# The first half-step of a decoder block on x with features on partitions: the norm's roots moved from x to the products' results

## The chip, the cores and the metric

The kernel runs on one core of a Trainium2 chip. The metric is the device time of one execution in microseconds (us). Times come from three runs of the kernel before and from one profiled execution of it. TensorE multiplies (PE, with PEld its weight loads), VectorE is DVE, ScalarE is ACT, GpSimd is POOL, and SyncE (SP) issues most transfers.

## The reference

One decoder block on x of 1024 tokens by 1024 features, float32. Only its first half-step is touched by the change:

```python
def rms_norm(x, g):
    y = xf * lax.rsqrt(jnp.mean(xf * xf, axis=-1, keepdims=True) + RMS_EPS)
    return y * g

def swiglu(x, w1, w3, w2):
    return (jax.nn.silu(x @ w1) * (x @ w3)) @ w2

# h = x + 1/2 * swiglu(rms_norm(x, g1), w1a, w3a, w2a)     D = 1024, D_FF = 2816
# then: u = rms_norm(h, g2) @ W_in, attention and pooling, gates, W_o, a second half-step, a last norm
```

The root of a token's mean square is one number for each token. It can be applied to the token's row of x, or, since `x @ w` is linear, to the results for that token.

## The kernel before

Every product is float32 split in two parts (high and low, type fp32r), three matmuls for one: high by high, high by low, low by high (`three`, `Sevens.product`). A product of 512 x 512 x 512 is 12 matmuls of 128x128 by 128x512.

The up-projections of a half-step are done with seven products in place of eight (`Quad`, L336): a pair of column blocks of w1 (A) and w3 (B) times x gives four quarters from seven products, numbered 1 to 7. Each takes one sum of x's quarters: `b11`, `b21`, `b22` (quarters of normed x by halves of tokens and of features), and `t1` to `t4`, sums of quarters. `Quad.operand` (L349) sums the weight's quarters on VectorE and splits the result: ACT writes the high part, GpSimd (or, for each third one, VectorE) the low part (`split`, L318). `Quad.run` (L388) issues the 12 matmuls; products 1 and 2 of a quad add up in one PSUM bank, 3 and 5 in another. `Pair.a_out` and `Pair.b_out` (L600, L629) take the results: for A the function (`Silu`) on ACT, for B the multiplication into A's result on VectorE. There are 11 pairs.

Normed x must have its features on partitions for the products. `begin_up1` (L981) loads rows of x (tokens on partitions), takes squares on ACT (`squares`), the inverse root on VectorE and GpSimd (`inverse`, a power of -0.5), scales the rows on VectorE, and turns them on TensorE, four 128x128 transposes into one bank (`Rows`, L402, and `turned`, L487). From the bank, ACT writes the high part and VectorE the low part. The gains are turned too (`gains`), and so are the roots (`means`).

While the first rows come, four products of the later pairs 4 and 5 (`led`) run on a first quarter of x that comes from memory with features on partitions already (`x_t`, unscaled but for the gain), and their results are scaled (`led_scaled`), stored and fetched when pairs 4 and 5 need them. Then come products 1 and 2 of pairs 0 to 2, with the transposes of rows 4 to 7 between them (`Entry.run`). After this opening, `up` (L696) runs products 6, 7, 5, 4 and 3 of the pairs begun, and then the pairs 3 to 10; an operand is prepared two products ahead.

The opening and the first part of `up` stand under `tc.manual_schedule()`: each engine has its instructions in the order of the code, written out by hand. The pairs 3 to 9 are ordered by the planner. SP's queue issues the transfers in the order of `load_all` and of `raws.load`.

`Down.add` (L871) adds the results of the down-projection to h with a factor of plus or minus one half.

Of the kernel before, what the change touches and what calls it, by code (L numbers as in the profile page):

```python
# [16 lines left out]
P = 128  # L17
# [120 lines left out]
def tile_block(  # L138
# [53 lines left out]
    consts.tile([P, 24], F32, name="pad")  # L192
# [3 lines left out]
    consts.tile([P, 32], F32, name="pad2")  # L196
# [87 lines left out]
    def scaled_part(t, c, gain):  # L284
        ve.scalar_tensor_tensor(h[t][:, c], h[t][:, c], inv[t][:, 1:2], gain[:, c], op0=OP.mult, op1=OP.mult)

# [19 lines left out]
    class Sevens:  # L306


        def __init__(self, name, X, fw, fs=None):
            self.name, self.X, self.fw, self.fs = name, X, fw, fs or fw  # L310
            self.n_lo = 0
            self.terms = (0, 1, 2)
            self.led = {}
# [251 lines left out]
    class Pair:  # L565
# [3 lines left out]
        def __init__(self, sv, j, sums, early=False, spare=False):  # L569
# [3 lines left out]
            self.place_of = [h_tile if spare else tmp, h_tile if early else tmp]  # L573
            self.u2 = (lambda n: h_tile(f"u2_{n}")[:, :HALF]) if spare else (lambda n: sv.half_tile("u", n))
# [5 lines left out]

        def place(self, row, cols):
            while len(self.y) <= row:
                self.y.append(self.place_of[len(self.y)](f"y_{self.sv.name}{self.j}_{len(self.y)}"))
            return self.y[row][:, cols]
# [5 lines left out]
        def fetch_b(self):  # L590
            if self.led is not None:
                self.u[2] = self.u2(f"{self.j}2")
                nc.sync.dma_start(self.u[2], self.led[1])

# [6 lines left out]
        def a_out(self, m, p):  # L601
            lows, highs = slice(0, HALF), slice(HALF, S)

            u2 = self.place(0, highs)
            if m == 1:
# [3 lines left out]
            elif m == 2:  # L609
                c = self.place(0, lows)  # L610
                if self.led is not None:
                    ve.tensor_tensor(c, p, u2, op=OP.add)
                    p = c
                ac.activation(c, p, AF.Silu)
            elif m == 7:
                ve.tensor_tensor(self.place(1, lows), p, u2, op=OP.add)
            elif m == 5:
                c22 = self.place(1, highs)
                ve.tensor_tensor(c22, p, self.place(1, lows), op=OP.add)
                ac.activation(c22, c22, AF.Silu)  # L620
            elif m == 4:
                u3 = self.place(1, lows)
                ve.scalar_tensor_tensor(u3, p, -1.0, u3, op0=OP.mult, op1=OP.add)
                ac.activation(u3, u3, AF.Silu)
            else:
                ve.tensor_tensor(u2, p, u2, op=OP.add)
                ac.activation(u2, u2, AF.Silu)

        def b_out(self, m, p):  # L629
            lows, highs = slice(0, HALF), slice(HALF, S)  # L630
            u, j = self.u, self.j
            if m == 1:
# [24 lines left out]
            else:  # L657
                ve.tensor_tensor(u[2], p, u[2], op=OP.add)
                d = self.place(0, highs)
                ve.tensor_tensor(d, d, u[2], op=OP.mult)  # L660

# [116 lines left out]
    class Down:  # L778
# [3 lines left out]
        def __init__(self, name, sums, half_tile, pair):  # L782
# [7 lines left out]
            self.right, self.apart = {}, set()  # L790
            downs.append(self)
# [137 lines left out]
    X = sums_of_x(scope.enter_context(sbuf("x1")), "f1", SUMS)  # L929

    for t in range(NT):
        h.append(h_tile(f"x{t}"))

    def load_rows(*ts):
        for t in ts:
            nc.sync.dma_start(h[t], x[t * P:(t + 1) * P, :])

    gain_row = keep.tile([P, D], F32, tag="gain", bufs=1, name="gain_ffn1")
    led_x, led_in = [], []
    for n in range(2):  # L940
        led_x.append(row(f"led_x{n}").rearrange("p (k c) -> p k c", k=2))
        led_in.append(row(f"led_w{n}").rearrange("p (k c) -> p k c", k=2))
    square = X["t1"][0][:, 0:2, :].rearrange("p k c -> p (k c)")
    square2 = tmp("square2")

    LED = (4, 5)
    led_dram = [dram.tile([P, HALF], F32, name=f"led{q}") for q in range(4)]

    def load_all():
        def features(kk):  # L950
            nc.sync.dma_start(led_x[kk], x_t[0, kk])

        def weight(q):
            nc.sync.dma_start(led_in[q // 2][:, q % 2], (w1a, w3a)[q % 2][2 * LED[q // 2]][:, LOWS])

        features(0)
        weight(0)
        weight(1)
        features(1)
        load_rows(0)  # L960
        weight(2)
        load_rows(1)
        weight(3)
        load_rows(2, 3)
        raws.depth = 2
        raws.load()
        load_rows(4)
        raws.depth = 3
        raws.load()
# [1541 lines left out]
```

## Time and profile before

| | us |
|---|---|
| median of 3 runs | 1884.19 (1883.82 to 1884.75) |
| profiled execution | 1884.1 |
| its span | 1882.3 |
| TensorE busy in the span | 1872.2 (99%) |
| VectorE busy | 1349.0 (72%) |
| ACT busy | 773.4 (41%) |
| GpSimd busy | 727.7 (39%) |

The span is what the profiler sees of the program; the rest of the time lies around it. A busy TensorE is one with matmuls in flight, whose ends are modelled; the start-to-start distance of matmuls tells their rate. Idle time of the other engines matters only where TensorE waits for them.

### The profile page before, as it was taken

The numbers are of one execution on the slowest core, as the hardware profiler recorded it, in microseconds if no ns is written. First come the engines' busy times: TensorE is split into PE (matmuls) and PEld (weight loads), VectorE is DVE, ScalarE is ACT, GpSimd is POOL, SyncE is SP. The second block draws the span as 40 slices with busy tenths as digits, with TensorE's granted clock in tenths as the row PEclk, the third lists the DMA queues.
The fourth block names the chain that finished last, engine by engine and source line by source line (L and its number), as shares of the span: only waits on it lengthen the run. The fifth ranks groups of instructions, "written<-read, shape, count | busy, mean of one in ns | idle before, by whom it ended". The sixth has DMA issues, their size and how long they took to land.

```text
span 1882.3 us, 24614 instructions
## 1 busy us (share of the span) xinstructions
PE 1872.2 (99%) x8758; PEld 1554.8 (83%) x8758; DVE 1349.0 (72%) x1981; ACT 773.4 (41%) x1395; POOL 727.7 (39%) x543
## 2 busy tenths in 40 slices
PE   9999999999999999999999999999999999999998
PEld 8888888888888888888888888888888888888886
DVE  7877666558786776658885897787765566577867
ACT  7433333334344543334445772363333333334344
POOL 4533333331223364444554457545333333312221
PEclk9999999999999999999999999999999999999999
DMA  6154323336565526765578878634332233354654
GB/s 248 56 201 163 128 100 116 115 118 222 177 224 196 182 91 221 243 219 188 209 254 315 313 227 294 262 147 172 125 139 85 89 107 111 136 200 156 225 197 146
DMA packets 146035, 334.98 MB, mean 178 GB/s; under 512 B 17784, under 2 KB 39288, under 8 KB 144376
## 3 DMA queue, kind: packets, MB, share of 16 engines
q1 hardware_dynamic: 142168, 322.55, 49.7%
q10 hardware_dynamic: 3744, 10.85, 1.6%
q8 instruction: 69, 1.13, 0.2%
q14 instruction: 54, 0.44, 0.1%
HBM read 232.76 MB, written 100.60 MB: 177 GB/s over the span
## 4 chain that ended last, share of the span: by engine, by line
PE 54%; DVE 3%; ACT 2%; issue 1%; DMA 1%; POOL 1%; ACTq 0%; SPq 0%; DVEq 0%; POOLq 0%
PE u_mixm L332 15%; PE d_f L869 8%; PE wo L2191 4%; PE yp L1933 1%; PE u_f20a L332 1%; PE u_f21b L332 1%; PE u_f20b L332 1%; PE u_f21a L332 1%; PE u_f210b L332 1%; PE u_f210a L332 1%; PE u_f29b L332 1%; PE u_f29a L332 1%; PE u_f28b L332 1%; PE u_f28a L332 1%; PE u_f27b L332 1%
## 5 line engine op out<-in xcount | busy, mean ns | idle before, releaser
L869 PE MATMUL d_f<-bhi_f,ahi_f 128*128 128x512 f32 x616 | 240.2, 390 | 0.0
L869 PE MATMUL d_f<-bhi_f,alo_f 128*128 128x512 f32 x616 | 239.7, 389 | 0.0
L869 PE MATMUL d_f<-blo_f,ahi_f 128*128 128x512 f32 x616 | 239.6, 389 | 0.0
L826 POOL TENSOR_TENSOR alo_f<-g_f,ahi_f 128x512 fp32r<-128x512 f32 x60 | 86.0, 1450 | 273.6 <-ACT ahi_f L822 273.6
L332 PE MATMUL u_mixm<-xhi_t_mix,wc_mixm 128*128 128x512 f32 x608 | 157.3, 391 | 0.6 <-ACT wc_mixm L320 0.6
L869 PEld LDWEIGHTS d_f<-bhi_f,ahi_f 128*128 128x128 f32 x616 | 115.7, 188 | 24.1 <-ACT h L422 0.5
L869 PEld LDWEIGHTS d_f<-bhi_f,alo_f 128*128 128x128 f32 x616 | 115.6, 188 | 24.1
L869 PEld LDWEIGHTS d_f<-blo_f,ahi_f 128*128 128x128 f32 x616 | 115.7, 188 | 23.9
L332 PEld LDWEIGHTS u_mixm<-xhi_t_mix,wc_mixm 128*128 128x128 f32 x608 | 113.5, 188 | 24.4 <-ACT wc_mixm L320 1.1
L332 PE MATMUL u_mixm<-xhi_b_mix,wc_mixm 128*128 128x512 f32 x456 | 120.3, 391 | 0.0
L323 POOL TENSOR_TENSOR wc_mixm<-s_mixm,wc_mixm 128x512 fp32r<-128x512 f32 x52 | 77.1, 1483 | 102.1 <-ACT wc_mixm L320 102.1
L332 PEld LDWEIGHTS u_mixm<-xhi_b_mix,wc_mixm 128*128 128x128 f32 x456 | 85.0, 188 | 17.2
L320 ACT ACTIVATE wc_mixm<-s_mixm 128x512 fp32r<-128x512 f32 x76 | 47.0, 628 | 112.2 <-DVE s_mixm L376 57.2
L822 ACT ACTIVATE ahi_f<-g_f 128x1024 fp32r<-128x1024 f32 x84 | 81.9, 975 | 4.1 <-DMA g_f<-gs_f 4.1
L332 PE MATMUL u_mixm<-xlo_t_mix,wc_mixm 128*128 128x512 f32 x304 | 81.3, 389 | 0.0
L323 POOL TENSOR_TENSOR wc_mixm<-raw,wc_mixm 128x512 fp32r<-128x512 f32 x41 | 62.3, 1523 | 37.5 <-ACT wc_mixm L320 31.8
L2191 PE MATMUL wo<-w_o,o_hi 128*128 128x512 f32 x224 | 69.4, 391 | 0.1
L822 ACT ACTIVATE bhi_f<-s_f2w 128x512 fp32r<-128x512 f32 x55 | 32.9, 628 | 86.7 <-DVE s_f2w L844 67.8
L822 ACT ACTIVATE bhi_f<-s_f1w 128x512 fp32r<-128x512 f32 x55 | 33.0, 629 | 83.1 <-DVE s_f1w L844 69.9
L332 PEld LDWEIGHTS u_mixm<-xlo_t_mix,wc_mixm 128*128 128x128 f32 x304 | 57.1, 188 | 12.0
L826 DVE TENSOR_TENSOR alo_f<-g_f,ahi_f 128x1024 fp32r<-128x1024 f32 (+1 forms) x48 | 57.6, 1200 | 8.5 <-ACT ahi_f L822 8.5
L332 PE MATMUL u_mixm<-xlo_b_mix,wc_mixm 128*128 128x512 f32 x228 | 61.0, 389 | 0.0
(1359 smaller groups left out, 4768.1 us busy)
## 6 DMA issues: line engine op xcount, KB each, us to landing
g_f<-gs_f SPq DMA_DIRECT2D x70, 512.0 KB
gs_f<-y_f SPq DMA_DIRECT2D x88, 256.0 KB
raw<-in_w2a_dram SPq DMA_DIRECT2D x35, 512.0 KB
raw<-in_w2b_dram SPq DMA_DIRECT2D x35, 512.0 KB
gs_f<-gb_f SPq DMA_DIRECT2D x46, 256.0 KB
raw<-in_w1a_dram SPq DMA_DIRECT2D x22, 512.0 KB
raw<-in_w3a_dram SPq DMA_DIRECT2D x22, 512.0 KB
raw<-in_w1b_dram SPq DMA_DIRECT2D x22, 512.0 KB
```

Source lines behind the costliest of these rows:

```text
L320: ac.activation(w[:, 0], src, AF.Copy)
L323: eng.tensor_tensor(w[:, 1], src, w[:, 0].bitcast(F32), op=OP.subtract)
L332: pe.matmul(p, a, b, start=(start and n == 0), stop=(n == 11), skip_group_check=not start)
L822: ac.activation(hi[:, c], src, AF.Copy)
L826: eng.tensor_tensor(lo[:, d], src[:, o], hi[:, d].bitcast(F32), op=OP.subtract)
L869: pe.matmul(self.banks[m][t], l, r, start=(first and q == 0), stop=(last and q == 2))
L1933: pe.matmul(p, a, b, start=(j == 0), stop=(j == 11))
L2191: pe.matmul(banks[m][t], l, r, start=(st == 0 and j == 0 and q == 0), stop=(st == 1 and j == 1 and q == 2))
```

## The change

All of x comes from memory with features on partitions (`x_t`, eight transfers). The opening makes the seven sums from it without the roots: gains are vectors of one number per partition (`gain1`, `less` is their negative). No row of x is turned any more. The rows of x are still loaded, into tiles of their own, for the squares alone. The roots of each half of the tokens are turned once (`spread`, four transposes into one bank) and copied to `norm`, a tile with a token's root in every partition. For the first factor (A) the results are multiplied with `norm`: product 2's on VectorE, the others on GpSimd (`lit`), and the function follows when the next result is taken (`late`, `functions`). For the second factor (B) nothing is multiplied; its roots go into the factor of one half in `Down.add` (`halves`). The four products led run later, behind the first products of pairs 0 and 1, unscaled, and are copied out by ACT. The gain of the next norm is loaded behind `up`.

```diff
         def a_out(self, m, p):
...
-                    p = c
-                ac.activation(c, p, AF.Silu)
+                    self.lit(c, lows)
+                elif self.sv.norm is not None:
+                    ve.tensor_tensor(c, p, self.sv.norm[:, lows], op=OP.mult)
+                    self.late.append(c)
...
-                ac.activation(c22, c22, AF.Silu)
+                self.lit(c22, highs)
...
+        def lit(self, c, cols):
+            if self.sv.norm is not None:
+                gp.tensor_tensor(c, c, self.sv.norm[:, cols], op=OP.mult)
+                self.late.append(c)
+            else:
+                ac.activation(c, c, AF.Silu)
...
         def add(self, m, t):
...
-                ve.scalar_tensor_tensor(hs, self.banks[m][t], 0.5 * sign, hs, op0=OP.mult, op1=OP.add)
+                by = 0.5 * sign
+                if self.halves is not None:
+                    by = self.halves[sign][:, 4 * th + t:4 * th + t + 1]
+                ve.scalar_tensor_tensor(hs, self.banks[m][t], by, hs, op0=OP.mult, op1=OP.add)
...
+        features(0, 0)
+        weight(0, LOWS)
+        weight(1, LOWS)
+        features(0, 1)
+        weight(2, LOWS)
+        weight(3, LOWS)
+        features(0, 2)
+        led_weight(0)
+        features(0, 3)
+        led_weight(1)
+        features(1, 2)
+        features(1, 0)
+        led_weight(2)
+        led_weight(3)
+        features(1, 3)
+        features(1, 1)
+        load_rows(0, 1)
+        weight(0, HIGHS)
+        load_rows(2, 3)
+        for j in (1, 2, 3):
+            weight(j, HIGHS)
+        more(6)
+        load_rows(4, 5, 6, 7)
...
+        def first_sum(k):
+            ve.tensor_tensor(xt(1, k), xt(1, k), xt(0, k), op=OP.subtract)
+
+        def scaled_b22(k):
+            ve.tensor_scalar(xt(1, k + 4), xt(1, k + 4), gain(k + 4), None, op0=OP.mult)
+            high("b22", k, xt(1, k + 4))
+        def second_sum(k):
+            t2[k] = bank("acc", f"x_t2_{k}")
+            ve.scalar_tensor_tensor(t2[k], xt(1, k), less[:, k:k + 1], xt(1, k + 4), op0=OP.mult, op1=OP.add)
+            high("t2", k, t2[k])
...
+        def out(n, m):
+            outs[n](m, banks[n])
+            pairs[n // 2].functions()
...
+        for k in (4, 5):
+            high("b21", k, xt(0, k), gain(k), ve if k == 5 else ac)
+            low("b21", k, xt(0, k), gain(k))
+        run(2, 1)
+        out(1, 1)
+        led_high(1)
+        for k in (6, 7):
+            high("b21", k, xt(0, k), gain(k), ve if k == 7 else ac)
+            low("b21", k, xt(0, k), gain(k))
+        run(3, 1)
+        out(2, 1)
+        led_high(2)
+        for k in (0, 1):
+            scaled_b22(k)
+            first_sum(k)
+        led_run(0)
+        out(3, 1)
+        led_high(3)
+        for k in (0, 1):
+            low("b22", k, xt(1, k + 4))
+        for k in (2, 3):
+            scaled_b22(k)
+            first_sum(k)
+        led_run(1)
+        led_out(0)
+        operand(0, 2)
+        for k in (2, 3):
+            low("b22", k, xt(1, k + 4))
+        squares_of_x(0)
+        squares_of_x(1)
+        led_run(2)
+        led_out(1)
+        operand(1, 2)
+        squares_of_x(2)
+        squares_of_x(3)
+        led_run(3)
+        for k in (0, 1):
+            second_sum(k)
+            low("t2", k, t2[k])
+            third_sum(k)
+            fourth_sum(k)
+        inverses(0)
+        led_out(2)
+        operand(2, 2)
+        run(0, 2)
+        led_out(3)
+        operand(3, 2)
+        norm_p = bank("acc", "norm0")
+        second_sum(2)
+        low("t2", 2, t2[2])
+        third_sum(2)
+        fourth_sum(2)
+        half_roots(0)
+        run(1, 2)
+        p = spread(0, norm_p)
+        spread_copy(0, p)
+        second_sum(3)
+        low("t2", 3, t2[3])
+        third_sum(3)
+        fourth_sum(3)
+        out(0, 2)
+        operand(4, 1)
+        squares_of_x(4)
+        squares_of_x(5)
+        run(2, 2)
+        out(1, 2)
+        operand(5, 1)
+        squares_of_x(6)
+        squares_of_x(7)
...
+        out(2, 2)
+        more(8)
+        run(3, 2)
+        operand(4, 2)
+        inverses(1)
+        out(3, 2)
+        for k in (0, 1):
+            high("t3", k, xt(0, k), None, ac)
+            low("t3", k, xt(0, k))
+        run(4, 1)
+        out(4, 1)
+        operand(5, 2)
...
+        run(5, 1)
+        out(5, 1)
+        operand(0, 6)
+        half_roots(1)
...
+        run(4, 2)
+        p = spread(1)
+        operand(0, 7)
+        out(4, 2)
+        spread_copy(1, p)
+        for k in (2, 3):
+            high("t1", k, xt(1, k), gain(k))
+            low("t1", k, xt(1, k), gain(k))
+        run(5, 2)
+        out(5, 2)
+        for k in range(4):
+            high("t4", k, xt(0, k + 4))
+            low("t4", k, xt(0, k + 4))
         return pairs
```

## Rows read from the trace of the kernel before

**Rows 1.** The page: its first line and the engines' busy time.

```profile
span 1882.3 us, 24614 instructions
PE 1872.2 (99%) x8758; PEld 1554.8 (83%) x8758; DVE 1349.0 (72%) x1981; ACT 773.4 (41%) x1395; POOL 727.7 (39%) x543
```

**Rows 2.** TensorE's longest waits, whole run: us in total, times, longest.

```profile
PE idle L990 <- DVE mhalf L198: 1.1, 1, 1.1
PE u_mixm L332 <- ACT wc_mixm L320: 0.6, 1, 0.6
```

**Rows 3.** Time line of TensorE in the opening: start, duration, what.

```profile
6.38 0.73 PE L1048 MATMUL u_led<-xhi_t_f,wc_led 128*128 128x512 f32 x2
...
33.38 1.07 PE L332 MATMUL u_f10a<-xhi_b_f,wc_f10a 128*128 128x512 f32 x4
...
36.10 0.60 PE L487 MATMUL x_b<-ident,x 128*128 128x128 f32 x4
...
58.78 1.21 PE L332 MATMUL u_f10a<-xhi_t_f,wc_f10a 128*128 128x512 f32 x4
```

**Rows 4.** Groups of TensorE's transposes, 0 to 140 us: busy us, mean ns.

```profile
L411 PE MATMUL x_b<-ident,x 128*128 128x128 f32 x48 | 6.9, 273 | 0.0
...
L487 PE MATMUL x_b<-ident,x 128*128 128x128 f32 x16 | 2.4, 272 | 0.0
L994 PE MATMUL gain<-ident,gain 128*128 128x128 f32 x8 | 1.0, 272 | 0.0
L994 PE MATMUL means<-ident,nst 128*128 128x128 f32 x4 | 0.6, 272 | 0.0
```

**Rows 5.** Time line of ACT.

```profile
9.45 1.06 ACT L274 ACTIVATE xhi_t_f<-x 128x1024 fp32r<-128x1024 f32 x1
...
10.51 0.62 ACT L1030 ACTIVATE wc_led<-led_w 128x512 fp32r<-128x512 f32 x1
11.03 0.58 ACT L1001 ACTIVATE gain_ffn<-gain 128x512 f32<-128x512 f32 x1
11.69 1.07 ACT L274 ACTIVATE xhi_t_f<-x 128x1024 fp32r<-128x1024 f32 x1
```

**Rows 6.** Time line of VectorE.

```profile
4.50 0.49 DVE L1020 TENSOR_SCALAR xhi_t_f<-led_x,gain 128x512 fp32r<-128x512 f32 x1 [3.49 <-DMA gain<-in_ffn_norm_dram]
5.25 1.41 DVE L1023 SCALAR_TENSOR_TENSOR xlo_t_f<-led_x,gain,xhi_t_f 128x512 fp32r<-128x512 f32 x2 [0.27 <-ACT xhi_t_f L1018]
...
42.01 0.68 DVE L438 TENSOR_TENSOR xlo_t_f<-x_b,xhi_t_f 128x512 fp32r<-128x512 f32 x1
42.61 0.68 DVE L480 TENSOR_TENSOR x<-x_t,x 128x512 f32<-128x512 f32 x1
```

**Rows 7.** Time line of GpSimd.

```profile
10.88 0.55 POOL L279 TENSOR_TENSOR nst<-nst,mhalf 128x1 f32<-128x1 f32 x1 [1.35 <-DVE nst L278]
11.40 1.30 POOL L1034 TENSOR_TENSOR wc_led<-led_w,wc_led 128x512 fp32r<-128x512 f32 x1
```

**Rows 8.** VectorE beside GpSimd: a time line's row, and L652 (min/median/max ns).

```profile
8.91 1.82 DVE L1023 SCALAR_TENSOR_TENSOR xlo_t_f<-led_x,gain,xhi_t_f 128x512 fp32r<-128x512 f32 x2
...
L652 DVE TENSOR_TENSOR y_f<-y_f,u_f x22: 684/692/1824, 81.6 to 1661.0; 128x512 f32<-128x512 f32 x22
```

**Rows 9.** Busy time by windows: PE, PEld, DVE, ACT, POOL, clock, DMA.

```profile
100.00:200.00 100.00, 100.00 (x443) 82.81 (x442) 72.14 (x97) 31.15 (x51) 36.20 (x26) 1.00 0.52 179
420.00:640.00 220.00, 219.96 (x989) 182.18 (x988) 172.71 (x218) 96.20 (x136) 54.02 (x39) 1.00 0.61 202
```

**Rows 10.** The mixer's gain: its readers and its transfer, first and last start.

```profile
L282 DVE SCALAR_TENSOR_TENSOR h<-h,nst,gain_mix x4: 1273/1278/2318, 599.2 to 625.3; 128x1024 f32<-128x1024 f32 x4
...
L204 ACTq DMA_DIRECT2D gain_mix<-in_mix_norm_dram x1: 335/335/335, 53.9 to 53.9; - x1
```

**Rows 11.** Transfers, 0 to 60 us in slices of 1.5 us.

```profile
GB/s 0 203 291 316 378 350 367 406 426 412 415 407 415 404 418 396 401 407 412 216 14 0 347 3 0 0 0 11 0 71 284 112 238 0 0 0 123 227 0 0
```

**Rows 12.** Tail windows (clock before DMA), and the first matmuls (min/median/max ns).

```profile
1875.00:1882.30 7.30, 0.16 (x1) 0.00 (x0) 2.60 (x6) 2.94 (x7) 1.10 (x2) 0.83 0.65 241
...
L990 PE MATMUL idle<-ones x26: 275/421/582, 1.1 to 6.3; 128*128 128x128 f32 x26
```

More of the change, by code (lines that the diff above doesn't have):

```diff
@@ L312, in __init__ @@
             self.terms = (0, 1, 2)
+            self.norm = None
             self.led = {}
@@ L939, in tile_block @@
[L939 to L947, printed above, removed]
[L949 to L975 removed]
+            nc.sync.dma_start(rows_of_x[t], x[t * P:(t + 1) * P, :])
@@ L984, in begin_up1 @@
         load_all()
+        sv1.norm = norm
         idle = bank("mm", "idle")
-        def keep_on(n):
-            for _ in range(n):
-                pe.matmul(idle[:, :P], ones, ones, start=True, stop=True)
-        def spread(p, columns):
-            for k, c in enumerate(columns):
-                pe.transpose(p[:, k * P:(k + 1) * P], c.to_broadcast([P, P]), ident)
-            return p
-        def gains(b):
-            return spread(bank("acc", f"gain{b}"), [gain1[:, k:k + 1] for k in range(4 * b, 4 * b + 4)])
@@ L1037, in begin_up1 @@
-        count = {}
-        def led_run(q, ks, terms):
-            w = led_w[q]
-            if q not in led_p:
-                led_p[q] = bank("mm", f"u_led{q}")
-                count[q] = 0
+        for _ in range(13):
+            pe.matmul(idle[:, :P], ones, ones, start=True, stop=True)
+        ve.memset(fours, -0.5)
+        ve.tensor_scalar(less, gain1, -1.0, None, op0=OP.mult)
+        pairs = [Pair(sv1, j, sums, True, (lambda n: u2_last[:, :HALF]) if j == 2 else None) for j in range(3)]
@@ L1094, in begin_up1 @@
-        first_scaled(1)
-        squares(2, square)
-        squares(3, square)
-        r[0].lower()
-        inverse(2)
-        led_run(2, range(4), (0, 1))
-        rows(1, "b11", LOWS, "acc", ve)
-        first_scaled(2)
-        inverse(3)
-        led_run(2, range(4), (2,))
-        pairs = [Pair(sv1, j, sums, True, j == 2) for j in range(3)]
-        entry = pre_run(sv1, [(q, m) for m in (1, 2) for q in pairs[:2]] + [(pairs[2], m) for m in (1, 2)],
-                        pairs[0], h[:4])
@@ L1141, in begin_up1 @@
-        squares(4, square2)
-        entry.operand(3)
-        inverse(4)
-        r[2].lower()
-        entry.product(2)
-        entry.out(1)
-        r[3].lower()
-        entry.operand(4)
-        squares(5, square2)
-        for t in range(4):
-            r[t].keep(h[t][:, HIGHS])
-        entry.product(3)
-        entry.out(2)
-        entry.operand(5)
-        entry.out(3)
-        for q in (0, 1):
-            led_scaled(q)
-        def high(t, part):
-            if part == 0:
-                inverse(t)
-                return
-            scaled(t, h[t], gain_row)
-            return h[t]
@@ L1166, in after @@
-        def after(t):
-            if t + 2 < NT:
-                squares(t + 2, square2)
-            if t < 6:
-                raws.depth = t + 3
-                raws.load()
-        entry.run(high, after, 4)
+                    a, b = three((w[:, 0, r], w[:, 1, r]), (hi[:, k, :], lo[:, k, :]))[i]
+                    pe.matmul(banks[n], a, b, start=(k == 0 and i == 0), stop=(k == 3 and i == terms[-1]))
+        FRONT, BACK = slice(0, 2 * P), slice(2 * P, HALF)
+        high("b11", 0, xt(0, 0), gain(0))
```

287 lines of the change are left out of this document (157 added, 130 removed).

## The prediction

> **What bounds the kernel now.** I read the page first, then the waits, then time lines of the opening. TensorE has work in 1872.2 of 1882.3 us [rows 1], and in the whole run its longest wait after the start is 0.6 us, far behind the part that changes [rows 2]. So before a change can save time it must take instructions off TensorE, and it loses time as soon as TensorE has to wait. The median of the runs is 1884.19 us; the profiled execution took 1884.1 us, 1.8 us of it outside the span. I add to 1884.1.
>
> **What comes off TensorE.** The 16 products of the opening (12 matmuls each) and the transposes between them run from 6.38 us to 58.78 us, 52.40 us [rows 3]. A product alone takes 36.10 - 33.38 = 2.72 us [rows 3], so 16 take 43.5. The remaining 8.9 us belong to 76 transposes (48 + 16 + 8 + 4) [rows 4], groups of four or eight that also slow the matmul behind them. The change keeps 8, for the roots (`spread`, twice four): 8.9 x 8/76 = 0.9. It takes off 8.0 us. The matmuls stay as many, only reordered, and the first still waits for the same two transfers.
>
> **What must be ready in their place.** The transposes were also time in which ACT, VectorE and GpSimd got ahead. The opening would be 44.4 us long; I laid the new order end to end, each engine in the order of the code, which ACT keeps in [rows 5] (square, split, gain copy, square). Prices: ACT 0.52 us from one 512-column instruction to the next and 1.06 a square [rows 5]; VectorE 0.60, 0.66 with a vector of gains, 0.45 from one source (0.49 long, less the overlap of the others) [rows 6]; GpSimd 1.30 a subtraction, 0.55 a power [rows 7]; 0.03 to 0.08 for each hand-over.
>
> First, the small wait W0. The second half of the first product needs `low` for k = 3, which ended at 8.91 + 1.82 = 10.73 [rows 8] and comes no earlier; without the gain transposes TensorE is there at 10.3: 0.4.
>
> W1, the norm. `spread(0)` stands behind the tenth product, which ends at 6.38 + 27.2 + 0.4 = 34.0. Its roots come so. (a) ACT copies the first product out at 11.1, splits a led weight and writes b21's fourth high part: VectorE begins at 13.0. (b) VectorE has 15 instructions up to the last scaled b22: 4 x 0.66 + 6 x 0.45 + 5 x 0.60 = 8.3, with hand-overs 8.6. All have only SBUF operands, and GpSimd makes the lower parts of the led weights in this time. Where a VectorE instruction with two SBUF sources met a GpSimd subtraction it took 1.824 instead of 0.692 us, up to 1.1 more [rows 8]; three or four such meetings here: 2.9 more. So 24.5. (c) ACT then has five instructions and four squares, 5 x 0.52 + 4 x 1.06 = 6.8: 31.3. (d) Only then does t2's first high part stand on ACT, and `inverses(0)` stands on VectorE behind both t2 blocks: high 0.60, low 0.60, third and fourth sum 1.32, next second sum 0.74, high 0.60, low 0.60, two sums 1.32, inverse 0.14, power 0.55, hand-overs 0.4: 6.9. (GpSimd's power stands ahead of the split of (2, 2), which is due 5 us later.) Roots at 38.2, and a wait of 4.2, bounded by 1.7 (no meeting in b, slightly quicker hand-overs) and 5.0 (each of the four costs its full 1.1). I take 3.9, the end with meetings, because (b) is dense with the kind of row 8.
>
> W2, operand (4, 1). In ACT's order its split stands behind the function of pair 0, which needs `out(0, 2)`, which stands on VectorE behind the third and fourth t2 blocks. From `inverses(0)`: 0.74 + 0.60 + 0.60 + 1.32 + 0.25 + 0.74 + 0.60 + 0.60 + 1.32 + 0.68 on VectorE and ACT in turn, function 0.52, split 0.62, hand-overs 0.3: 8.9. TensorE meanwhile has power and hand-over 0.7, transposes 0.45, two products 5.44: 6.6. Wait 2.2.
>
> W3, product (4, 2). It adds into the bank of (4, 1), which ACT must copy first. Behind the split of (4, 1) ACT has four squares 4.24, splits 1.04, a function 0.52, two highs 1.04, the copy 0.60, with the split's own 0.52: 8.0. TensorE needs 0.7 + 5.44. Wait 1.9.
>
> W4, pair 0's next products. Product 7 needs sums that VectorE makes between t1's lows: 0.7. Product 5's split stands on ACT behind a function, a copy, two t1 highs and four t4 highs, 5.3 us from the split of product 7, TensorE needing 3.3 from there: 2.0. Product 3 needs a bank read out: 0.4. Together 3.1, between 1.2 without meetings and 4.
>
> Sum: 0.4 + 3.9 + 2.2 + 1.9 + 3.1 = 11.5 us of new waits against 8.0 us gained, **3.5 us longer**. With the lower ends, 0.1 + 1.7 + 2.2 + 1.9 + 1.2 = 7.1, 0.9 shorter; with the upper ends, 0.5 + 5.0 + 2.3 + 2.0 + 4.0 = 13.8, 5.8 longer.
>
> The Trainium skill, "SBUF — State Buffer", section "Who interferes with whom", has an exclusive lock here: VectorE and GpSimd share a port pair, and whoever issues second is blocked until the other ends. By the rule in full the meeting on the row would have cost about GpSimd's whole 1.3 instead of 1.1; W1 would go to its upper end, the sum to 12.6 and the time to 1888.7.
>
> **Edits at nothing, and their cover.** Roots on the results: GpSimd multiplies 35 results (33 and two for the led pairs), at 1.30 us 45 us over the 360 us of the half-step; it is busy 36 of 100 us there and VectorE 72 [rows 9], and TensorE waits nowhere in that stretch. VectorE gets nine more products of 0.68, 6 us. If the cover went, one product in each of eight later pairs would wait for one GpSimd instruction: 8 x 1.3 = 10 us. Operands are prepared two products (5.4 us) ahead and functions come one result later, so I take 0. The half roots in `add`: 48 instructions that read a vector instead of a number, 0.06 each (0.66 against 0.60), 3 us in a stretch where VectorE is idle 47 of 220 us [rows 9]: 0. The mixer's gain, loaded at 53.94 us before and first used at 599 us [rows 10], is loaded about 175 us ahead: 0. Transfers: 3 MB more of x on SP's queue. The last rows for the first roots are byte 8.7 million of it; the queue had moved that much by 24.8 us [rows 11], their squares come at 29 to 31: 0, and 0.5 if the half-wide weight transfers run slower. SP's later transfers wait behind raw 7 for a place that t1 frees at about 61 us; nothing behind it is due before 70: 0.
>
> **The rivals.** (A) As summed: 1884.1 + 3.5 = 1887.6, from 1886 to 1889.3. (B) The GpSimd subtractions mostly miss VectorE's instructions, because ACT releases them in VectorE's gaps: W1 and W4 shrink to their lower ends or halfway, 1883.2 to 1886. For it: of 22 such instructions on the row the median is the short time [rows 8]. Against: in (b) VectorE has no gaps. (C) The cover holds, because ACT or VectorE reaches the roots before 34 us and the split before 40: at most 8.0 less, 1876 to 1880.3. Against: W2 and W3 are made of instructions counted in order and don't hang on any meeting. (D) Slower, by the clock: TensorE's granted clock falls in W1's gap. That it falls after idleness is seen once: TensorE ended at 1875.2, and the last 7.3 us have a mean of 0.83 [rows 12]. It decides if W1's gap is long enough for that; what is long enough no row inside the kernel shows, but W1 is 3.9 to 5.0 us and the tail's idle stretch 7.1. The price: at the start the 26 matmul records on `ones` took a median of 421 ns against 275 once the clock had risen, at the lower level for most of their 5.3 us [rows 12]; half speed for as long again costs 2.6 more, less what W2 then hides (up to 2.2): 1888 to 1890.5, more if W2 and W3 let it fall again. "TensorE: Matmul & The Clock Gate" of the Trainium skill, section "HAM oscillation", names waits between groups of matmuls as what halves the clock again and again; no row shows it inside this kernel.
>
> **How the numbers follow.** A measurement here tells about 0.2% (3.8 us) from no change. A 0.55: its middle lies just inside the bound, so I split it 0.30 same and 0.25 slower. B 0.20, same. C 0.10, faster. D 0.15, slower. Faster 0.10, same 0.50, slower 0.40. Predicted 1887.6. The range from 1881.5 to 1890.5 takes in A, B and half of D, leaving out C and the rest of D, under 2 in 10.
>
> **What would show it.** Right: TensorE idle before the roots' transposes (released by GpSimd's power), before (4, 1) (by ACT's split), before (4, 2) (by ACT's copy) and before pair 0's product 5, some 11 us in the first 75, and none up to 420; 8 transposes left. Wrong: waits under 4 us in the opening (C); waits in later pairs behind GpSimd's multiplications; a granted clock under 1 there (D).

## The result, and the profile after

| | before | after |
|---|---|---|
| median, us | 1884.19 | 1893.3 |
| profiled execution, us | 1884.1 | 1892.72 |
| its span, us | 1882.3 | 1890.5 |
| start of the opening's last part (first matmul on t2), us | 58.78 | 61.39 |
| the same matmul of pair 0's second factor, us | 72.55 | 78.20 |
| first product of the second matrix (`d_f`), us | 434.31 | 443.65 |

The change makes the kernel slower: ratio 1.0048, interval 1.0033 to 1.0063. That is 9.1 us by the medians and 8.6 by the profiled executions; 1887.6 was predicted, and the time lies outside the range.

The page of after, first line and busy times, answering to [rows 1]. TensorE has 68 instructions fewer and is busy 2.1 us less; the span is 8.2 us longer.

```profile
span 1890.5 us, 24508 instructions
PE 1870.1 (99%) x8690; PEld 1548.8 (82%) x8690; DVE 1371.3 (73%) x1979; ACT 765.5 (40%) x1385; POOL 775.9 (41%) x566
```

TensorE's longest waits in the whole run (us in total, times, longest), answering to [rows 2]:

```profile
PE norm L1107 <- POOL roots L1101: 5.0, 1, 5.0
PE u_first L1150 <- DVE xlo_b_f L1056: 1.2, 1, 1.2
...
PE u_f10a L334 <- DVE xlo_t_f L1054: 0.7, 1, 0.7
PE u_f13a L334 <- DVE y_f L627: 0.7, 1, 0.7
PE u_f10a L334 <- DVE y_f L627: 0.6, 1, 0.6
PE u_f16b L334 <- ACT u_f L657: 0.6, 1, 0.6
PE u_f19b L334 <- ACT u_f L657: 0.6, 1, 0.6
PE u_f17b L334 <- ACT u_f L657: 0.5, 1, 0.5
PE u_f12a L334 <- ACT y_f L610: 0.5, 1, 0.5
```

The first, second and last are W1, W0 and W3, the `u_f10a` ones belong to W4 (products 4 and 3 of pair 0). Those of `u_f13a`, `u_f16b`, `u_f17b` and `u_f19b` lie in the later pairs, where none was expected. A wait in this view is a little shorter than the gap in starts; from here on I give gaps (start to start, less the usual 0.227 us).

The time line of TensorE (start, duration, what), answering to [rows 3]: the tenth product, the roots' transposes, the eleventh product, product (4, 2), and the opening's end. A pair of numbers (n, m) stands for product m of quad n; quads 0 and 1 are the two factors of pair 0, quads 4 and 5 those of pair 2.

```profile
34.33 1.07 PE L334 MATMUL u_first<-xhi_b_f,wc_f10b 128*128 128x512 f32 x4
40.42 1.12 PE L1107 MATMUL norm<-ident,roots 128*128 128x128 f32 x4 [5.03 <-POOL roots L1101]
41.19 2.06 PE L334 MATMUL u_f11a<-xhi_b_f,wc_f11a 128*128 128x512 f32 x4
43.05 1.91 PE L334 MATMUL u_f11a<-xlo_b_f,wc_f11a 128*128 128x512 f32 x4
44.75 1.87 PE L334 MATMUL u_f11a<-xhi_b_f,wc_f11a 128*128 128x512 f32 x4
...
55.35 1.20 PE L334 MATMUL u_f12a<-xhi_b_f,wc_f12a 128*128 128x512 f32 x4 [0.53 <-ACT y_f L610]
...
61.39 1.07 PE L334 MATMUL u_f10a<-xhi_t_f,wc_f10a 128*128 128x512 f32 x4
```

Four matmuls take 1.9 to 2.1 us instead of 1.07: the product from 41.19 to 46.46 lasts 5.27 us, 2.55 more than usual. The windows of the same stretch (PE, PEld, DVE, ACT, POOL, clock, DMA) show why: after 4 us without a matmul the granted clock is at 0.50, the lower of its two levels (1.2 of 2.4 GHz).

```profile
36.00:40.00 4.00, 0.00 (x0) 0.00 (x0) 2.84 (x6) 3.07 (x6) 1.02 (x1) 0.95 0.48 152
40.00:44.00 4.00, 3.58 (x11) 3.00 (x12) 3.44 (x6) 1.09 (x3) 2.84 (x3) 0.50 0.34 123
```

What made the roots late, step by step: time-line rows of VectorE, ACT and GpSimd.

```profile
9.02 2.68 DVE L1056 SCALAR_TENSOR_TENSOR xlo_b_f<-x_t,gain,xhi_b_f 128x512 fp32r<-128x512 f32 x2
14.05 1.28 DVE L1056 SCALAR_TENSOR_TENSOR xlo_b_f<-x_t,gain,xhi_b_f 128x512 fp32r<-128x512 f32 x1 [2.35 <-ACT xhi_b_f L1047]
...
23.55 0.48 DVE L1062 TENSOR_SCALAR x_t<-x_t,gain 128x512 f32<-128x512 f32 x1
...
24.55 1.52 DVE L1062 TENSOR_SCALAR x_t<-x_t,gain 128x512 f32<-128x512 f32 x1
...
32.80 0.58 ACT L1047 ACTIVATE xhi_t_f<-x_t 128x512 fp32r<-128x512 f32 x1
...
38.98 1.39 POOL L1101 TENSOR_TENSOR roots<-means,fours 128x4 f32<-128x4 f32 x1 [6.74 <-DVE means L1100]
```

The two lows of the first row set W0: 2.68 us where [rows 8] had 1.82, since two subtractions of GpSimd (9.64 to 12.85) now stand back to back there. From 14.05 on VectorE works without a pause to the last scaling, which ends at 26.07. The same scaling takes 0.48 us at 23.55 and 1.52 at 24.55: both lie beside one GpSimd subtraction (23.58 to 25.78), the first begins 0.03 us before it, the second within it. And the power of four columns takes 1.39 us where one took 0.55 [rows 7].

One of the later waits, before product 2 of the second factor at 275.88:

```profile
272.14 1.29 POOL L325 TENSOR_TENSOR wc_f16b<-s_f16b,wc_f16b 128x512 fp32r<-128x512 f32 x1 [1.33 <-ACT wc_f16b L322]
273.39 1.29 POOL L646 TENSOR_TENSOR y_f<-y_f,norm_ffn 128x512 f32<-128x512 f32 x1
274.71 0.63 ACT L642 ACTIVATE y_f<-y_f 128x512 f32<-128x512 f32 x1 [2.71 <-POOL y_f L646]
275.25 0.58 ACT L657 ACTIVATE u_f<-u_f16b 128x512 f32<-128x512 f32 x1
275.88 1.20 PE L334 MATMUL u_f16b<-xhi_b_f,wc_f16b 128*128 128x512 f32 x4 [0.60 <-ACT u_f L657]
```

The chain is read from below. TensorE waits for ACT's copy, which empties the bank that product 2 adds into. The copy's source had been complete since about 272.6, but ahead of it in ACT's queue stands the function, and the function waits for GpSimd's product with the roots' row, which stands behind the low part of a split.

### The profile page after: what moved, and what is told of

The parts are those of the page before. It is cut to its first block, busy times and chain, and to the rows that moved or that the text cites. A ratio compares the mean times of both kernels' runs of the same rounds, so it can differ in the third digit from the quotient of the medians.

```text
span 1890.5 us, 24508 instructions
## 1 busy us (share of the span) xinstructions
PE 1870.1 (99%) x8690; PEld 1548.8 (82%) x8690; DVE 1371.3 (73%) x1979; ACT 765.5 (40%) x1385; POOL 775.9 (41%) x566
## 4 chain that ended last, share of the span: by engine, by line
PE 54%; DVE 3%; ACT 2%; issue 1%; DMA 1%; POOL 1%; ACTq 0%; SPq 0%; DVEq 0%; POOLq 0%
PE u_mixm L334 15%; PE d_f L894 8%; PE wo L2315 4%; PE yp L2057 1%; PE u_f20a L334 1%; PE u_f21b L334 1%; PE u_f20b L334 1%; PE u_f21a L334 1%; PE u_f210b L334 1%; PE u_f210a L334 1%; PE u_f29b L334 1%; PE u_f29a L334 1%; PE u_f28b L334 1%; PE u_f28a L334 1%; PE u_f27b L334 1%
## 5 line engine op out<-in xcount | busy, mean ns | idle before, releaser
L847 ACT ACTIVATE bhi_f<-s_f1w 128x512 fp32r<-128x512 f32 x55 | 33.1, 629 | 83.5 <-DVE s_f1w L869 70.7
```

What stands on the lines that cost most here:

```text
L847: ac.activation(hi[:, c], src, AF.Copy)
```

## The experiments

**Sum or chain?** The prediction added up waits as if each stood for itself. The rival reading: one chain of work on VectorE and ACT runs from 26 to 60 us, and TensorE's waits are only the places where it meets that chain. The first run moves one link, the second fills TensorE's gap.

e1_roots_early:

```diff
         for k in (0, 1):
             second_sum(k)
+            if k == 0:
+                inverses(0)
             low("t2", k, t2[k])
             third_sum(k)
             fourth_sum(k)
-        inverses(0)
```

> Two theories of the opening. The sum (the prediction's way): each wait of TensorE and each stretch at the lower clock counts for itself, so a wait taken away is time given back, less what the next one hides. The chain: from about 26 us VectorE and ScalarE work through one queue of sums, squares, roots, norm rows, functions and splits without slack, and TensorE waits wherever it meets it, so that a wait taken away in one place comes back in the next. Here VectorE's step and GpSimd's power of the first roots come right behind the first second sum, not behind two sums with all that belongs to them; nothing is left out. The roots should be there at 34.5 instead of 40.4, and the wait before the transposes shrinks from 5.2 to about 2.0 us, the bank then being the last (ScalarE's copy of the third led product frees it at 37.2). The sum: clock stays high (2.9 back), wait 3.2 less, product (4,1) waits 2.2 and (4,2) 1.2 more; the opening ends at 58.7 instead of 61.39, total 1890.6. The chain: (4,1) waits 4 to 5 us, the opening ends at 60.9 to 61.4, total 1892.8 to 1893.3.

Measured: 1892.19 us, the opening's end at 61.20. TensorE's waits:

```profile
PE u_f12a L334 <- ACT wc_f12a L322: 2.6, 1, 2.6
PE norm L1107 <- issue: 1.9, 1, 1.9
```

The roots no longer bind; the first gap is 2.06, before the same transposes, and the rest comes back as 2.71 before (4, 1). The clock still fell, twice for 3.4 us. The opening's end lies where the chain has it; the total is 0.6 us below the chain's and 1.6 above the sum's, which counted on a clock that stays up.

e2_no_clock_fall (the move of the copy in the first loop, then the filler):

```diff
             fourth_sum(k)
+            if k == 0:
+                led_out(2)
         inverses(0)
-        led_out(2)
 ...
         run(1, 2)
+        for _ in range(23):
+            pe.matmul(norm_p[:, :P], ones, ones, start=True, stop=True)
         p = spread(0, norm_p)
```

> The price of the clock alone: the wait before the roots' transposes is filled with 23 idle matmuls of 0.21 us into the bank that the transposes fill anyway; so that this bank is free, ScalarE's copy of the third led product stands between the first two highs of t2, where ScalarE waits 2.7 us. Nothing is left out. The clock should stay at its higher level through 39.6 to 46.5. The sum: 2.9 us back for the product at half speed, less 2.2 for product (4,1) and 1.2 for (4,2), which then wait again: the opening ends at 60.9, total 1892.8. The chain: (4,1) waits 2.5 to 3 us and (4,2) 1.9 instead of 0.7, the opening ends at 61.0 to 61.4, total within 0.5 us of 1893.3. If the clock's fall costs its full 2.9 us: 58.5 and 1890.4.

Measured: 1894.39 us, the opening's end at 61.77. The window that stood at 0.50 in after:

```profile
40.00:44.00 4.00, 4.00 (x27) 3.57 (x26) 3.46 (x6) 1.08 (x2) 3.22 (x3) 1.00 0.29 114
```

TensorE's waits:

```profile
PE u_f12a L334 <- ACT y_f L610: 1.5, 1, 1.5
PE u_f12a L334 <- ACT wc_f12a L322: 1.3, 1, 1.3
```

The tenth product's last third, the transposes and the opening's end in e2:

```profile
34.73 1.07 PE L334 MATMUL u_first<-xhi_b_f,wc_f10b 128*128 128x512 f32 x4
...
41.07 0.60 PE L1107 MATMUL norm<-ident,roots 128*128 128x128 f32 x4
...
61.77 1.07 PE L334 MATMUL u_f10a<-xhi_t_f,wc_f10a 128*128 128x512 f32 x4
```

The clock stays at 1.00, the eleventh product takes its usual time, and nothing is gained: TensorE now waits 1.49 us before (4, 1) and 1.63 before (4, 2). The end came 0.4 later than after's because the chain began that much later in this execution: VectorE's first low of b21 starts at 14.41 instead of 14.05, the first high of t2 at 33.16 instead of 32.80. (The wait at 392 us was 0.45 longer; the total is 0.6 above what either theory allowed.) Both runs speak for the chain. From the end of its tenth product to the opening's end TensorE needs 61.39 - 35.24 = 26.15 us in after and 61.77 - 35.64 = 26.13 in e2. What it loses there is 5.19 + 0.35 + 2.55 (transposes and product at the lower clock) + 0.69 = 8.8 us in after and 5.43 (filled) + 1.49 + 1.63 = 8.6 in e2, however it is divided.

**What makes the chain late?** Two runs, one taking away GpSimd's reads beside VectorE, one taking the scalings off VectorE.

e4_led_lows_empty:

```diff
-            gp.tensor_tensor(led_w[q][:, 1], led_in[q], led_w[q][:, 0].bitcast(F32), op=OP.subtract)
+            gp.memset(led_w[q][:, 1].bitcast(F32), 0.0)
```

> The low parts of the four led operands are filled with zeros by GpSimd instead of subtracted, so that the led products lack their low part of the weights; TensorE's work is the same. GpSimd then reads nothing from SBUF for them. If VectorE is late in the opening because its scalings and subtractions meet GpSimd's subtractions (1.51 us for a scaling that takes 0.48 alone): the last scaling of b22 ends at 23.5 to 24.5 us instead of 26.07, the first high of t2 comes at 31 to 31.5 instead of 32.80, the wait before the roots' transposes is 1.5 us shorter, and the opening ends 1 to 2 us earlier, total 1891.3 to 1892.3. If the rows' landing or ScalarE's own work set these times: the first high of t2 stays at 32.5 or later, and total within 0.5 us of 1893.3.

Measured: 1889.8 us, the opening's end at 58.20. Time-line rows of VectorE's first low of b21, the last scaling, the first high of t2 and the opening's end:

```profile
12.99 0.75 DVE L1056 SCALAR_TENSOR_TENSOR xlo_b_f<-x_t,gain,xhi_b_f 128x512 fp32r<-128x512 f32 x1 [2.38 <-ACT xhi_b_f L1047]
...
21.12 0.48 DVE L1062 TENSOR_SCALAR x_t<-x_t,gain 128x512 f32<-128x512 f32 x1
...
29.60 0.58 ACT L1047 ACTIVATE xhi_t_f<-x_t 128x512 fp32r<-128x512 f32 x1
...
58.20 1.07 PE L334 MATMUL u_f10a<-xhi_t_f,wc_f10a 128*128 128x512 f32 x4
```

The last scaling ends 4.5 us earlier (21.6 instead of 26.07) and the whole opening is 3.2 us earlier, more than expected. Not all of the 4.5 is the edit: VectorE's stretch also begins 1.06 us earlier (12.99 instead of 14.05), and the first fill comes only at 12.95. TensorE's first products were done earlier in this execution; W0 is 0.59 us here. The stretch itself shrinks from 12.0 to 8.6 us, so 3.4 us are VectorE's meetings with four GpSimd subtractions. At the opening's end they are worth 3.2 us against after, and 2.8 against e10 below, whose opening is after's and begins as early (first low at 13.05, end at 60.99); part is lost again where ACT waits 1.0 us for a transfer before the squares. Two scalings that begin within a fill take 0.57 and 0.63 us, one that begins before a fill 0.48; within a subtraction it was 1.51 to 1.52. The lows, with two sources, keep their 0.74 to 0.75 beside a fill. The Trainium skill ("SBUF — State Buffer", section "Who interferes with whom") states that a VectorE instruction with two SBUF inputs contends with a GpSimd instruction that reads SBUF, not with one that only writes, and that `tensor_scalar` can take the shared ports too. The trace agrees with both.

e5_scale_on_scalar:

```diff
-            ve.tensor_scalar(xt(1, k + 4), xt(1, k + 4), gain(k + 4), None, op0=OP.mult)
+            ac.activation(xt(1, k + 4), xt(1, k + 4), AF.Copy, scale=gain(k + 4))
```

> The chain theory, one link: the four scalings of x's b22 part by the gains go from VectorE (0.48 to 1.52 us each, beside GpSimd's led subtractions) to ScalarE, which waits there 3.3, 0.4, 0.6 and 1.4 us for them. Nothing is left out. Worked out with in-order queues from the durations of the trace of after: the first high of t2 comes about 3 us earlier than 32.80, the wait before the roots' transposes shrinks from 5.2 to about 2.5 us, and the opening ends at 58.2 instead of 61.39; total 1890.1. If a later link (squares, the landing of x's rows) sets the chain's pace: first high of t2 at 32 or later, total 1892.8 or more.

Measured: 1890.54 us, first high of t2 at 30.28, gap before the roots' transposes 2.52, opening's end 58.94 (58.2 expected). As the chain says: 2.5 us taken out at its head come off at its end, though gaps of 1.74 and 1.67 appear before (4, 1) and (4, 2).

**The later pairs.** e3_no_later_products:

```diff
-            if self.sv.norm is not None:
+            if self.sv.norm is not None and self.place_of[1] is h_tile:
                 gp.tensor_tensor(c, c, self.sv.norm[:, cols], op=OP.mult)
```

> GpSimd's products with the roots' rows are left out in the later pairs (from the fourth on, and in the products of pair 0 to 2 nothing is changed); the functions come at once behind VectorE's read. So those results lack the scaling. If these products are what makes later pairs wait (3.4 us between 78 and 630 us: a wait of 0.6 to 0.85 us before products at 163.5, 275.9, 314.8 and 391.8, ScalarE's function behind GpSimd's product, and behind that function the copy that frees the bank): these waits go, the gap between d_f and the opening falls by 3 to 3.5 us, total 1889.8 to 1890.3, and GpSimd is busy about 35 us of 100 instead of 48. If VectorE's nine added products or the added transfers make them: they stay, total 1892.8 to 1893.3. The opening is the same as after in both.

Measured: 1889.49 us, 3.8 less than after by the medians; in the trace the stretch from pair 0's second factor to `d_f` takes 362.8 us instead of 365.4, 2.6 less (3 to 3.5 expected). The medians say more because the profiled execution of this run is the longest of seven and that of after the shortest of five. TensorE's waits between 78 and 640 us:

```profile
PE u_f13a L334 <- DVE y_f L627: 0.7, 1, 0.7
```

A window of later pairs (columns as above):

```profile
200.00:300.00 100.00, 100.00 (x442) 82.80 (x442) 67.26 (x94) 31.18 (x51) 34.90 (x24) 1.00 0.34 115
```

Three of the four waits are gone (that of `u_f13a`, 0.84 us as a gap, stays in every run, the last ones included: there VectorE works without a pause up to its read of a bank at 162.68, one of the nine added products, 0.60 us from start to start, among it; what makes the wait was not tried apart), TensorE has work in 100.00 of 100 us, and GpSimd is back at 34.90. In after that window reads:

```profile
200.00:300.00 100.00, 99.40 (x439) 82.00 (x438) 78.28 (x94) 30.73 (x52) 48.15 (x33) 1.00 0.33 114
```

VectorE shows the same: as many instructions (94) take 78.28 us beside GpSimd's products and 67.26 without them.

e8_functions_later (the second list delays a function by one more product):

```diff
-            late, self.late = self.late, []
+            late = self.due()
+        def due(self):
+            late = self.late if self.place_of[1] is h_tile else self.older
+            self.older, self.late = self.late, []
+            return late
```

> Later pairs: after lets ScalarE apply the function one product behind GpSimd's product with the roots' row; here, from the fourth pair on, it is two products behind. The opening is as in after. If the waits at 275.9, 314.8 and 391.8 (0.70 to 0.76 us each) come from ScalarE standing in the function, with the copy behind it that frees the other factor's bank, they go: total 1891.0 to 1891.3; the wait at 163.5 stays, which is VectorE's read of a bank. If GpSimd's load itself (its low parts of the splits late) makes them: they stay, 1893.3.

Measured: 1894.04 us, the same three waits. Inconclusive: in these pairs a planner sets the order, and the trace still has the function (274.98) ahead of the copy (275.52). So the function was not delayed, and the run tells nothing of the two readings.

e10_third_on_vector:

```diff
-                self.lit(u2, highs)
+                self.lit(u2, highs, gp if self.place_of[1] is h_tile else ve)
```

> Later pairs: the last of a pair's four products with the roots' rows (product 3 of the first factor) goes from GpSimd, where it stands behind the low part of a split, to VectorE, right behind its read of the bank; from the fourth pair on. Nothing is left out, and the opening is as in after. If that product's lateness on GpSimd makes ScalarE's function late, and the function the copy behind it: the function is done some 2 us earlier, the waits at 275.9, 314.8 and 391.8 go, total 1890.5 to 1891.3, and only the wait at 163.5 is left. If the order of ScalarE's queue alone makes them, or VectorE has no room for eight more products of 0.7 us: as many waits, elsewhere, total 1892.8 to 1894.

Measured: 1891.42 us. ACT's function and copy in the stretch shown above:

```profile
272.58 0.62 ACT L642 ACTIVATE y_f<-y_f 128x512 f32<-128x512 f32 x1
273.28 0.60 ACT L657 ACTIVATE u_f<-u_f16b 128x512 f32<-128x512 f32 x1
```

The waits that are left between 78 and 640 us:

```profile
PE u_f13b L334 <- ACT u_f L657: 0.8, 1, 0.8
PE u_f13a L334 <- DVE y_f L627: 0.7, 1, 0.7
PE u_f18b L334 <- ACT u_f L657: 0.3, 1, 0.3
```

The function comes 2.1 us and the copy 2.0 us earlier, and the three waits go. But two others of the same kind appear elsewhere, so that the stretch from the second factor to `d_f` is only 0.9 us shorter. The profiled executions differ by 2.0; the other 1.1 lie in the opening (0.4), behind `d_f` (0.3) and outside the span (0.4), which the edit doesn't touch. With e3 this shows the cause of three of the four waits: ACT's queue behind a slow GpSimd product. Moving one of the four products shifts part of it.

**The chain as a matter of order.** e6_order has the instructions of after in another order; two pieces of it:

```diff
+        def tsum(k):
+            second_sum(k)
+            third_sum(k)
+            fourth_sum(k)
+            low("t2", k, t2[k])
 ...
         led_out(0)
-        operand(0, 2)
+        squares_of_x(0)
         for k in (2, 3):
             low("b22", k, xt(1, k + 4))
-        squares_of_x(0)
+        tsum(0)
         squares_of_x(1)
-        led_run(2)
-
         led_out(1)
+        operand(0, 2)
+        squares_of_x(2)
+        tsum(1)
         operand(1, 2)
-        squares_of_x(2)
         squares_of_x(3)
```

> The chain theory, the order of the queues: the same instructions as after, in another order from the fourth product's copy on. ScalarE: squares 0 to 3 between the highs of b22 and the splits, squares 4 to 7 one by one behind splits and copies that TensorE waits for, the splits of (4,1), (0,7), (0,5) ahead of work that is due later. VectorE: second, third and fourth sum before the low part (which waits for ScalarE's high), the roots' step behind the second of the four. TensorE: the first roots' transposes ahead of the tenth product, the second ones behind (5,2). Worked out with in-order queues: TensorE waits 2 us at (0,2), 2 at the roots, 1.6 at product 3 of pair 0 and nowhere else; the opening ends at 55.5 instead of 61.39 and pair 0's first quad at 70.7 instead of 78.2, total 1885.8. If the engines' work and not its order sets the opening's end (no order helps): 61 and 1893.

Measured: 1890.89 us. The opening's end came at 56.48, near the 55.5 expected, but pair 0's second factor only at 75.72 instead of 70.7: product 3 waited 2.3 us for VectorE, and behind that gap the clock fell for 3.4 us. So the order alone moves the opening's end by 4.9 us, but the total is 5.1 above the one worked out and only 2.4 under after.

e9_all adds e5 and e8 to it:

> The three edits together (scalings on ScalarE, the new order, functions two products behind in later pairs). Worked out with in-order queues: waits of 1.1 us at the roots and 1.6 at product 3 of pair 0, the first quad of pair 0 ends at 67.7 instead of 78.2 (72.55 before the change), and of the later waits about 1.4 us are left: total 1880 to 1881.5, under both kernels. If the sum theory is right and the engines have no slack to give: 1886 or more.

Measured: 1888.34 us, opening's end 55.21, second factor at 72.99 (expected 67.7). Its trace shows what was left out of the reckoning: gaps of 1.2 us before the first product and 1.3 within the first two (W0), 2.4 before the roots' transposes, which the new order had put ahead of the tenth product, 2.3 before product 3, and all of the later waits, since e8's edit has no effect. The total lies where the sum theory was given it (1886 or more), so the total does not speak for the chain here; the opening's end does, 6.2 us ahead of after's.

e11_refined (e9 without e8, with e10 and these moves):

```diff
-        run_first(0, (2, 3), (0, 2, 1))
-        run_first(1, (2, 3), (0, 2, 1))
+        for terms in ((0, 2), (1,)):
+            run_first(0, (2, 3), terms)
+            run_first(1, (2, 3), terms)
 ...
+        operand(0, 4)
+        operand(0, 3)
```

> The chain theory carried on: scalings on ScalarE and the new order, with four further moves of whole instructions: the first roots' transposes behind the tenth product again (their wait was 2.4 us ahead of it), the first products' low parts of x behind both factors' other terms (0.9 us more time for VectorE), the highs of t1 and the splits for product 5, 4 and 3 of pair 0 ahead of outputs that nothing waits for, the low part of product 3's split on GpSimd, the second roots' step behind the lows of t3; and in later pairs the product with the roots' row of e10. Nothing is left out. The chain: no wait at the roots, at most 0.5 in the first product's second half, 1 to 1.5 in pair 0; pair 0's first quad ends at 67 to 69 (72.55 before the change), later waits 1 to 1.5; total 1879.5 to 1882. If VectorE's and ScalarE's work (and not its order) is what is left: the quad ends at 72 or later and total is 1885 or more.

Measured: 1885.25 us, ratio 1.0005 (0.9996 to 1.0013): level with before. W0 is gone and the second factor starts at 70.52; four gaps are left (0.9, 1.9, 2.3 and 0.9 us). The total is 3.3 us above the chain's range and just within the other reading's (1885 or more); the second factor is not (72 or later). The profiled execution, 1883.71 us, is the shortest of eleven, so these gaps account for less than the median shows.

e12_best, its core, against e11:

```diff
         led_out(0)
+        operand(0, 2)
         squares_of_x(0)
...
         out(1, 2)
-        tsum(3)
-        half_roots(0)
-        squares_of_x(4)
         run(2, 2)
 
-        operand(5, 1)
         out(2, 2)
+        operand(5, 1)
+        tsum(3)
+        squares_of_x(4)
         squares_of_x(5)
```

> The version of the last run with the waits taken up that its trace still shows (0.9 before (0,2), 1.9 before (4,2), 2.3 before the second roots' transposes, 0.9 before a product of pair 3 that was new with the product on VectorE): the split of (0,2) ahead of the first square, the sums for pair 1's function ahead of the fourth second sum and squares 4 and 5 behind them, the copy of (4,1) behind square 6 where its product ends, the second roots' step ahead of the lows of t3 again, pair 3's last product with the roots' row on GpSimd again, both half roots at the end. Nothing is left out. The chain theory: these four waits go and the later ones are 0.8 to 1.4 us, the opening's first quad ends at 66 to 67.5 (72.55 before the change), total 1878.5 to 1881. If what is left is work and not order: the waits move to pair 0's products, the quad ends at 70 or later, total 1883 or more.

Measured: 1882.12 us, ratio 0.9988 (0.9979 to 0.9997): 2.4 us under before in the same comparison, 11 us under after, 1.1 above the chain's range and 0.9 below the other reading's (1883 or more). Its page:

```profile
span 1880.9 us, 24502 instructions
```

TensorE's longest waits:

```profile
PE u_f10a L334 <- DVE y_f L627: 1.2, 1, 1.2
...
PE u_first L334 <- ACT wc_f10b L322: 0.9, 1, 0.9
PE u_f13a L334 <- DVE y_f L627: 0.7, 1, 0.7
PE u_f10a L334 <- ACT wc_f10a L322: 0.6, 1, 0.6
```

The second factor starts at 69.25 (expected 66 to 67.5): the wait before product 3 of pair 0 stayed. TensorE does the same work as in after (8690 matmuls in both); what differs is where instructions stand, and the engine of the four scalings, of one low part in pair 0 and of one product in seven later pairs.

## Why the prediction was wrong

The direction was right, and so was the mechanism at the opening's head: TensorE waits for the roots, and for the reasons given. The size was not. Two of the prediction's own signs of being wrong came, waits in later pairs behind GpSimd's multiplications and a granted clock under 1; two of its signs of being right did not, the waits before (4, 1) and before pair 0's product 5. The account, in us on the profiled executions:

| term | predicted | measured |
|---|---|---|
| opening without waits (measured: 61.39 - 6.31 - 1.39 - 8.78) | 44.4 | 44.9 |
| W0 | 0.4 | 1.4 |
| W1 to W3 and the clock (5.19 + 0.35 + 2.55 + 0.69) | 8.0 | 8.8 |
| W4 (from the opening's end to the second factor: 16.81 less before's 13.78) | 3.1 | 3.0 |
| later pairs, up to `d_f` (9.34 less 5.65) | 0 | 3.7 |
| behind `d_f`, and outside the span (2.2 against 1.8) | 0 | -0.7 |

Together 5.1 us more than forecast, as 1892.72 stands to 1887.6. (Behind 640 us after has 2.05 us of small gaps where before has 2.77, which is most of the last row.)

- **The step that failed: "operands are prepared two products ahead and functions come one result later, so I take 0".** It is 3.7 of the 5.1 us; without it the time would have been 1889.0, inside the range. Cover was judged by load: GpSimd busy 36 of 100 us in [rows 9]. GpSimd did get its room (53.8 us of 100 between 100 and 200 us). What had no room was ACT's queue: the function was made to wait for GpSimd, and a copy that frees a bank stands behind it. For the opening the prediction counted what stands in ACT's queue ahead of a copy; here it did not. Its price if the cover went was 10 us; e3 puts the products at 2.6 us by the trace and 3.8 by the medians. Another 0.84 us is the wait of `u_f13a`, behind a VectorE queue that holds one of the nine added products; its cause stays open.
- **W0**: "comes no earlier" than 10.73 was read from a row of before; it came 1.0 us later, because in the new order GpSimd's two splits stand beside both lows. One row's duration was taken over into other company. W0 is no fixed price either: in e10, whose opening is after's, the two lows took 2.01 us, TensorE's first two products lost 1.1 us less, and the opening ended only 0.4 us earlier, since W1 (5.77) and W3 (1.67) grew.
- **W1**: (a) 13.0 was 14.05; (b) 24.5 was 26.07; (c) 6.8 was 6.7; (d) 6.9 was 7.6, of which the power's excess is 0.84 (1.39 for 0.55). With TensorE free at 35.2 instead of 34.0 the wait became 5.2, just over the upper bound. The bounds don't come out of the prediction's own terms: 4.2 without the 2.9 for meetings is 1.3, not 1.7, and four meetings at 1.1 make 5.7, not 5.0. The meetings in (b) were rightly seen as the main cause: 2.9 predicted, 3.4 by e4, where the stretch took just the 8.6 us counted without them.
- **W2 and W3** as waits of their own: wrong in kind. In after W2 is no wait at all and W3 0.7; in e2, with the clock held up, they are 1.5 and 1.6. The sum came close because it followed one chain from link to link: the roots came 2.2 us later than predicted (40.4 instead of 38.2), and the opening ended 2.2 later than predicted (61.4 instead of 6.38 + 44.4 + 0.4 + 8.0 = 59.2). Its parts can't be saved one by one. (W2's own numbers give 8.9 - 6.6 = 2.3, not 2.2.)
- **Rival D** happened and cost nothing in after: its 2.6 was measured as 2.55 and was hidden whole, as e2 shows. "Less what W2 then hides" should have included W3. Where no later link hides it a fall may cost: of e6's four executions the one with a mean granted clock of 1.000 took 1889.13 us, the three with 0.998 took 1890.78 to 1891.26.
- **Rival B**: the subtractions did not miss VectorE's instructions. Had they, e4 shows what it would have been worth: 2.8 to 3.2 us in the opening, within the 1.6 to 4.4 that B has, and 1889.8 in all, since W0 and the later pairs add theirs. **Rival C** found no cover in any run with after's order.
- **The 8.0 us gained** held within half a microsecond. **W4** held in sum by luck: before product 7 the gap was 0.67 us (0.7 predicted), before product 5 nothing (2.0), within product 4, which was not foreseen, 0.85 and 0.38 behind t4's lows, before product 3 0.81 (0.4).

## What to carry to other kernels

When a wait is put on an engine's queue, look for the cover of what stands behind it, not for the load of the engine it waits for: GpSimd had half its time free, and a 0.58 us copy behind ACT's function still held up TensorE. Where several waits of one engine hang on the same pair of other engines, ask whether they are one chain: here time was won at its head (less work, fewer meetings, another order) and not at the place where the wait was seen. A change that takes work off the bound engine may need its queues laid out anew to pay: here nearly the same instructions gave 1893.3 us in one order and, with four scalings, one low part and seven products on other engines, 1882.1 in another.

## What the runs showed of the hardware

- A power on GpSimd of 128x4 took 1.39 us in after's first use (1.02 to 1.51 over all runs), of 128x1 0.55 [rows 7]: four columns are far from free there.
- VectorE's scaling with one SBUF source (0.48 us) is held up by a GpSimd subtraction as much as one with two sources [rows 8]: 1.51 to 1.52 us when it begins within the subtraction, 0.48 when it began just before (23.55 in after). Beside GpSimd's fills it takes 0.48 to 0.63.
- The granted clock did not follow the length of the last gap alone: it fell around gaps of 2.06 and 2.71 us in e1, and stayed at 1.00 through gaps of 2.52, 1.74 and 1.67 us in e5. What tells the two apart stays open. The window of e1 around the first of its gaps:

```profile
36.00:42.00 6.00, 4.50 (x15) 3.61 (x16) 4.67 (x8) 3.69 (x7) 2.97 (x2) 0.72 0.52 179
```

The same window of e5:

```profile
36.00:42.00 6.00, 4.10 (x20) 3.48 (x21) 4.67 (x10) 2.00 (x4) 3.89 (x3) 1.00 0.51 169
```
